# A decoder layer on one core: the residual kept by tokens, down and output projections with the weights as the moving operand

## The chip, the cores and the metric

One NeuronCore of one Trainium2 chip runs the kernel. The metric is the device time of one execution in microseconds; three runs are shown, and their median counts. Besides the runs there is one profiled execution, from which all rows come.

## The reference

256 tokens (T), model width 2048 (D), feed-forward width 5632 (FF), 16 heads of 128, all float32:

```python
x = x + 0.5 * swiglu(rms_norm(x, ffn1_norm), w_gate1, w_up1, w_down1)
h = rms_norm(x, mix_norm);  z = h @ w_in            # q|k|v|B|C|xt|gate_attn|gate_conv
y_a = moba(q, k, v) @ w_attn_out                    # 256 tokens are one block: plain causal ALiBi attention
y_c = (B * causal_conv3(C * xt)) @ w_conv_out
x = x + (sigmoid(g_a) * y_a + sigmoid(g_c) * y_c) @ w_out
x = x + 0.5 * swiglu(rms_norm(x, ffn2_norm), w_gate2, w_up2, w_down2)
out = rms_norm(x, final_norm)
swiglu(h, g, u, d) = (silu(h @ g) * (h @ u)) @ d
```

## The kernel before, in words

Everything is kept transposed: `x` is [128, 16, 256], 16 tiles of 128 features by 256 tokens. Weights (some 460 MB) come from HBM once, in chunks of 512 KB: 128 partitions by 1024 numbers (CK = 8 K tiles of 128 outputs).

Each operand of a product is cut into a part rounded to the type float32r and a rest. `cut` does it for a weight chunk: ScalarE casts `w` to `hi` (L509), VectorE writes `lo = w - hi` (L510). For the activations `split_col` writes both parts side by side into 512 columns: `xn` (normed x), `at` (attention output) and `ring` (hidden activations of the feed-forward blocks, and the inputs of `wco` and `wo`).

- `job` (L158, L159) computes one tile of 128 outputs by 256 tokens. For each K tile: the stationary `hi` times all 512 columns (main part and correction), then the stationary `lo` times the first 256.
- `v_step` (L372 to L374) does the other form, since attention needs v by tokens: for each K tile and each 128 tokens the rounded activations are stationary and 512 columns of `hi`, then of `lo`, stream by; then the activations' rest is stationary with `hi` again. It has two banks of PSUM.
- `ffn` walks three rounds of hidden tiles, ROUNDS = (0,12), (12,28), (28,44): gate and up jobs fill `ring`, then 16 down jobs per round add half their result to `x[:, m, :]`. In the last round `finish_x` squares the tile for the next norm and splits it into `xn`.
- `mixer` runs the conv part, `conv_out`, attention (`v_step`, `stage_qk`, `stage_t`, `stage_pv`), `attn_out`, and 16 jobs of `wo`.
- `norm_cols` sums the squares over features with matmuls against `ones` (L121) and forms 1/sqrt; `norm_row` spreads that along the free axis. The factor is applied after the next matmul.

The order is written out by hand: `steps` is a list, and the loop at the end issues it. For each chunk it issues loads up to 7 chunks ahead on SP's queue (five `w` buffers), cuts up to 4 ahead (four `hi`, four `lo`), then the chunk's matmuls, and then one entry of `pending`, the post-processing of the job before. A step without chunks and without a `hold` flushes all of `pending` first:

```python
if not n:
    if s.hold is None:
        flush()
    s.pe(None)
    continue
```

One such step stands at the second tile of a last round and loads ScalarE's table for Sqrt.

Of the kernel before, what the change touches and what calls it, by code (L numbers as in the profile page):

```python
# [8 lines left out]
F32 = mybir.dt.float32  # L9
# [5 lines left out]
P = 128  # L15
# [9 lines left out]
ROUNDS = ((0, 12), (12, 28), (28, 44))  # L25
RING = 18
LOAD_AHEAD = 6
SPLIT_AHEAD = 4
NEG = -3.0e38

G1, GM, G2, GF, BG, CV = 0, 16, 32, 48, 64, 96
NCST = 144


class Step:
    def __init__(self, chunks, pe, post=None, hold=None):
        self.hold = hold
        self.chunks = chunks
        self.pe = pe
        self.post = post  # L40


@with_exitstack
def macaron_kernel(ctx: ExitStack, tc: tile.TileContext, xT, cst, wg1, wu1, wd1, win, wv, wao,
                   wco, wo, wg2, wu2, wd2, out):
# [69 lines left out]
    def norm_cols(tag):
        """1 / sqrt(mean(x^2) + eps) of token i * 128 + p in rcol[tag][p, i]."""
        ps = patt.tile([P, 4 * P], F32, name="psS", tag="psS")
        a = acc.pop(tag)
        for i in range(2):
            for j, t in enumerate(a):  # L120
                nc.tensor.matmul(ps[:, i:i + 1], t[:, i * P:(i + 1) * P], ones, start=(j == 0), stop=(j == 1))  # L121
# [92 lines left out]
    def prepare(k0, k1):  # L214
        for k in range(k0, k1):
            split_col(xn[:, k, :], x[:, k, :], vec(G1, k))

    def ffn(tag, wg, wu, wd, gain_next, next_tag, first=False):
# [4 lines left out]
        def gu(t):  # L223
# [27 lines left out]
        for r, (k0, k1) in enumerate(ROUNDS):  # L251
# [5 lines left out]
            last = r == len(ROUNDS) - 1  # L257
            for m in range(ND):
                def post(ps, m=m, last=last):
                    c = tmp("c")  # L260
                    nc.scalar.mul(c, ps[:, T:2 * T], 0.5)
                    nc.vector.tensor_add(c, c, x[:, m, :])
                    nc.vector.scalar_tensor_tensor(x[:, m, :], ps[:, 0:T], 0.5, c, op0=ALU.mult, op1=ALU.add)  # L263
                    if last:
                        finish_x(m, gain_next, next_tag)
                src = wd[m][:, k0 * P:k1 * P]
                nk = k1 - k0
                ch = [(src[:, k * P:min(k + CK, nk) * P], min(CK, nk - k)) for k in range(0, nk, CK)]
                if last and m == 1:
                    steps.append(Step([], lambda _: nc.scalar.preload_act_table(AF.Sqrt)))  # L270
                steps.append(job((tag, "d", r, m), ch, lambda k, k0=k0: ring((k0 + k) % RING), post))

    def finish_x(m, gain, tag):
        add_square(tag, m)
        if tag == "fin":
            nc.vector.tensor_scalar(sacc[:, m, :], x[:, m, :], vec(GF, m), None, op0=ALU.mult)
        else:
            split_col(xn[:, m, :], x[:, m, :], vec(gain, m))

    def mixer(gain_next, next_tag):  # L280
# [79 lines left out]
        def v_step(g):  # L360
# [18 lines left out]
            def post():  # L379
# [97 lines left out]

        for m in range(ND):
            def post(ps, m=m):
                c = tmp("c")  # L480
                nc.scalar.copy(c, ps[:, T:2 * T])
                nc.vector.tensor_add(c, c, x[:, m, :])
                nc.vector.tensor_add(x[:, m, :], ps[:, 0:T], c)
                finish_x(m, gain_next, next_tag)
            if m == 1:
# [93 lines left out]
_INS = ["xT", "cst", "wg1", "wu1", "wd1", "win", "wv", "wao", "wco", "wo", "wg2", "wu2", "wd2"]  # L579

# [35 lines left out]
```

## Time and profile before

| | us |
|---|---|
| median of 3 runs | 2513.7 |
| lowest and highest | 2513.22, 2515.71 |
| span of the profiled execution | 2511.6 |
| TensorE busy in that span | 2488.0 |

The span runs from the first to the last instruction of the profiled execution; the median stands 2.1 us above it. Spans of single matmuls are modelled and overlap, so the length of a stretch is read from where it begins and ends, not from the sum of its instructions.

### The profile page before, as it was taken

Reading aid. Unit: us, or ns where it says so; the run is one execution under the profiler, and the core shown is the slowest. Engines: PE = TensorE matmul, PEld = TensorE weight load, DVE = VectorE, ACT = ScalarE, POOL = GpSimd, SP = SyncE. Lnnn points to the kernel's source line nnn. Section 1 sums busy time; section 2 is a strip of 40 time slices with the busy share of each in tenths; the row PEclk is TensorE's granted clock in tenths of the full one; section 3 lists DMA queues with packets and bytes.
Section 4 is the critical chain, followed back from the end, with each engine's and each line's share of the span. In section 5 each row is a group of like instructions: output and inputs, shape, how many; then the busy total and the mean of one; then the engine's idle time right before and its main releaser. Section 6 shows DMA issues by size and latency. Waiting matters only on the chain.

```text
span 2511.6 us, 36296 instructions
## 1 busy us (share of the span) xinstructions
PE 2488.0 (99%) x14176; PEld 2181.3 (87%) x14176; DVE 1629.1 (65%) x2364; ACT 1206.7 (48%) x1807; POOL 1.9 (0%) x10
## 2 busy tenths in 40 slices
PE   8999999999999999999999999999999999999998
PEld 7888888888888888888888888888888888888886
DVE  6766666566677777655555566667666666656666
ACT  5544444444554444444444454455544444444443
POOL 0000000000000000000000000000000000000000
PEclk9999999999999999999999999999999999999999
DMA  6556566655665565556555545555555655656563
GB/s 219 196 177 205 185 192 190 188 187 191 188 189 185 185 198 189 192 187 190 177 169 183 168 164 192 189 188 189 186 192 171 204 189 191 190 187 191 187 189 121
DMA packets 131932, 468.02 MB, mean 186 GB/s; under 512 B 14640, under 2 KB 14768, under 8 KB 131760
## 3 DMA queue, kind: packets, MB, share of 16 engines
q1 hardware_dynamic: 131760, 465.70, 58.1%
q8 instruction: 111, 1.82, 0.3%
q14 instruction: 61, 0.50, 0.1%
HBM read 463.54 MB, written 2.10 MB: 185 GB/s over the span
## 4 chain that ended last, share of the span: by engine, by line
PE 98%; DVE 1%; DMA 1%; issue 0%; ACT 0%; SPq 0%; DVEq 0%; ACTq 0%
PE ps L158 62%; PE ps L159 32%; PE pv L374 1%; PE pv L373 1%; PE pv L372 1%; DMA w<-in_wu 0%; DMA w<-in_wg 0%; PE psS L395 0%; PE psV L429 0%; DVE lo L510 0%; PE psT L417 0%; DVE sacc L572 0%; PE psS L394 0%; PE psV L430 0%; PE psS L121 0%
## 5 line engine op out<-in xcount | busy, mean ns | idle before, releaser
L158 PE MATMUL ps<-xn,hi 128*128 128x512 f32 x4544 | 1583.6, 393 | 0.0
L510 DVE TENSOR_TENSOR lo<-w,hi 128x1024 fp32r<-128x1024 f32 (+1 forms) x904 | 1075.0, 1196 | 715.4 <-ACT hi L509 714.8
L159 PE MATMUL ps<-xn,lo 128*128 128x256 f32 x4544 | 1270.2, 280 | 0.0
L509 ACT CAST hi<-w 128x1024 fp32r<-128x1024 f32 (+1 forms) x904 | 921.6, 1024 | 605.5 <-PE ps L158 290.3
L158 PEld LDWEIGHTS ps<-xn,hi 128*128 128x128 f32 x4544 | 853.2, 188 | 187.5
L159 PEld LDWEIGHTS ps<-xn,lo 128*128 128x128 f32 x4544 | 853.1, 188 | 0.5
L158 PE MATMUL ps<-ring,hi 128*128 128x512 f32 x1920 | 674.9, 393 | 0.0
L159 PE MATMUL ps<-ring,lo 128*128 128x256 f32 x1920 | 543.0, 283 | 0.0
L158 PEld LDWEIGHTS ps<-ring,hi 128*128 128x128 f32 x1920 | 360.6, 188 | 83.3
L159 PEld LDWEIGHTS ps<-ring,lo 128*128 128x128 f32 x1920 | 360.9, 188 | 0.0
L172 DVE TENSOR_TENSOR t<-ps,c 128x256 f32<-128x256 f32 x320 | 133.9, 418 | 23.1 <-ACT c L170 23.1
L170 ACT COPY c<-ps 128x256 f32<-128x256 f32 x320 | 116.2, 363 | 54.5 <-PE ps L159 54.5
L87 ACT CAST ring<-hh 128x256 fp32r<-128x256 f32 x88 | 35.8, 407 | 200.3 <-DVE hh L235 200.3
L228 ACT ACTIVATE silu<-t 128x256 f32<-128x256 f32 x88 | 36.8, 418 | 157.3 <-DVE t L226 157.3
L158 PE MATMUL ps<-at,hi 128*128 128x512 f32 x256 | 89.5, 392 | 0.0
L159 PE MATMUL ps<-at,lo 128*128 128x256 f32 x256 | 71.6, 280 | 0.0
L88 DVE TENSOR_TENSOR ring<-hh,ring 128x256 fp32r<-128x256 f32 x88 | 37.5, 426 | 41.7 <-ACT ring L87 41.7
L110 ACT ACTIVATE sq<-x 128x256 f32<-128x256 f32 x56 | 22.3, 414 | 75.8 <-DVE x L263 50.1
L158 PEld LDWEIGHTS ps<-at,hi 128*128 128x128 f32 x256 | 48.1, 188 | 10.6
L374 PE MATMUL pv<-hi,xn 128*128 128x512 f32 x128 | 50.9, 398 | 0.0
L372 PE MATMUL pv<-hi,xn 128*128 128x512 f32 x128 | 50.7, 396 | 0.0
L373 PE MATMUL pv<-lo,xn 128*128 128x512 f32 x128 | 50.4, 394 | 0.0
(87 smaller groups left out, 850.3 us busy)
## 6 DMA issues: line engine op xcount, KB each, us to landing
w<-in_win SPq DMA_DIRECT2D x224, 512.0 KB, 4.0
w<-in_wg SPq DMA_DIRECT2D x172, 512.0 KB, 3.9
w<-in_wu SPq DMA_DIRECT2D x172, 512.0 KB, 3.8
w<-in_wd SPq DMA_DIRECT2D x160, 512.0 KB, 3.8
w<-in_wco SPq DMA_DIRECT2D x32, 512.0 KB, 3.9
w<-in_wv SPq DMA_DIRECT2D x32, 512.0 KB, 4.2
w<-in_wao SPq DMA_DIRECT2D x32, 512.0 KB, 4.2
w<-in_wo SPq DMA_DIRECT2D x32, 512.0 KB, 3.9
```

The costliest lines, as they stand in the source:

```text
L87: nc.scalar.copy(dst[:, 0:T], src)
L88: nc.vector.tensor_sub(dst[:, T:2 * T], src, f32(dst[:, 0:T]))
L158: nc.tensor.matmul(ps, hi[:, j * P:(j + 1) * P], r, start=(k == 0), stop=False)
L159: nc.tensor.matmul(ps[:, 0:T], lo[:, j * P:(j + 1) * P], r[:, 0:T], start=False, stop=(k == n - 1))
L170: nc.scalar.copy(c, ps[:, T:2 * T])
L172: nc.vector.tensor_add(t, ps[:, 0:T], c)
L228: nc.scalar.activation(s, g, AF.Silu)
L372: nc.tensor.matmul(pv[i], xh, hi[:, cols], start=(k == 0), stop=False)
L373: nc.tensor.matmul(pv[i], xh, lo[:, cols], start=False, stop=False)
L374: nc.tensor.matmul(pv[i], xl, hi[:, cols], start=False, stop=(k == ND - 1))
L509: nc.scalar.copy(hi[:, 0:nk * P], w)
L510: nc.vector.tensor_sub(lo[:, 0:nk * P], w, f32(hi[:, 0:nk * P]))
```

## The change

- `x` becomes token-major, [128, 2, 2048]. The transposed x that the first norm needs is loaded into `sacc`; the token-major one comes later, in four DMAs behind weight chunks 24, 26, 28 and 30.
- The down projections and `wo` no longer use `job` but `wide_job`: the form of `v_step`, four blocks (NB) of 512 outputs per round, `ring` stationary, the weights' `hi` and `lo` moving. Their weights are laid out for that in HBM (`blocks`), as `wv` is already.
- `residual` adds a block to `x` and squares it with `accum_out` (`row_square`), so that `norm_cols` sums rows on VectorE for the two inner norms and the final one. `turn` transposes a block of x back on TensorE, 8 transposes per block, and splits it into `xn`; the final norm needs none.
- The output is written by tokens, in four DMAs; the final gain comes as rows (`load_gain`, one buffer).
- Tiles are padded and shifted: `pad`, `padw`, a larger `ones`, T + 8 in `tmp`, chunks of 1024 + 128 numbers. Chunks for `job` start 24 numbers (96 bytes) into their `hi` and `lo`, chunks for `wide_job` and `v_step` at 0. `tmp` has 8 buffers instead of 10, `ring` 17 instead of 18. The first job after each change of `xn` has chunks of 4 K tiles.

The diff, cut to its core:

```diff
-RING = 18
+NW = 4 * P
+NB = D // NW
+X_LOAD = 24
+RING = 17
...
-G1, GM, G2, GF, BG, CV = 0, 16, 32, 48, 64, 96
-NCST = 144
+G1, GM, G2, BG, CV = 0, 16, 32, 48, 80
+NCST = 128
+LINE = 32
+SHIFT = 24
...
+    const.tile([P, 3 * LINE], F32, name="pad")
+    x = const.tile([P, 2, D], F32, name="x")
     xn = const.tile([P, ND, 2 * T], F32R, name="xn")
     at = const.tile([P, ND, 2 * T], F32R, name="at")
     sacc = const.tile([P, ND, T], F32, name="sacc")
+    xin = sacc
+    yout = sacc.rearrange("p a b -> p (a b)").rearrange("p (a b) -> p a b", b=D)
     cs = const.tile([P, NCST], F32, name="cs")
-    ones = const.tile([P, 1], F32, name="ones")
+    ones = const.tile([P, 4 * LINE], F32, name="ones")[:, 0:1]
     ident = const.tile([P, P], F32, name="ident")
     dist = const.tile([P, 3 * P], F32, name="dist")
+    work.tile([P, LINE], F32, name="padw", tag="padw", bufs=1)
...
-        t = work.tile([P, T + 2], F32, name=name, tag="tmp", bufs=10)
+        t = work.tile([P, T + 8], F32, name=name, tag="tmp", bufs=8)
...
+    ssq = {}
+    def row_square(tag, i, nb, junk):
+        if tag not in ssq:
+            ssq[tag] = work.tile([P, 2, NB], F32, name="ssq", tag="ssq", bufs=2)
+        nc.scalar.activation(junk, x[:, i, nb * NW:(nb + 1) * NW], AF.Square,
+                             accum_out=ssq[tag][:, i, nb:nb + 1])
...
+        if tag in acc:
...
+        else:
+            nc.vector.reduce_sum(s, ssq.pop(tag), axis=AX.X)
+            total = s
+        nc.vector.tensor_scalar(v, total, 1.0 / D, EPS, op0=ALU.mult, op1=ALU.add)
...
-    def pieces(w, m, nk=ND):
-        return [(w[m][:, k * P:min(k + CK, nk) * P], min(CK, nk - k)) for k in range(0, nk, CK)]
+    def pieces(w, m, ck=CK):
+        return [(w[m][:, k * P:(k + ck) * P], ck) for k in range(0, ND, ck)]
+    def wide(w, nb, k0=0, k1=ND):
+        return [(w[nb][:, k * NW:(k + 2) * NW], CK) for k in range(k0, k1, 2)]
...
+    def wide_job(chunks, src, post):
+        n = 2 * len(chunks)
+        held = []
+        def pe(parts):
+            pv = [psum_big("pv0"), psum_big("pv1")]
+            held.extend(pv)
+            k = 0
+            for hi, lo, _ in parts:
+                for j in range(2):
+                    cols = slice(j * NW, (j + 1) * NW)
+                    a = src(k)
+                    for i in range(2):
+                        xh = a[:, i * P:(i + 1) * P]
+                        xl = a[:, T + i * P:T + (i + 1) * P]
+                        nc.tensor.matmul(pv[i], xh, hi[:, cols], start=(k == 0), stop=False)
+                        nc.tensor.matmul(pv[i], xh, lo[:, cols], start=False, stop=False)
+                        nc.tensor.matmul(pv[i], xl, hi[:, cols], start=False, stop=(k == n - 1))
+                    k += 1
+                yield
+        return Step(chunks, pe, [lambda q=q: q(held) for q in post], shift=0)
+    def turn(nb, gain):
+        for half, tag in ((0, "psT"), (1, "psV")):
+            ps = patt.tile([P, 4 * P], F32, name=tag, tag=tag)
+            for c in range(2):
+                m = nb * 4 + half * 2 + c
+                for i in range(2):
+                    nc.tensor.transpose(ps[:, c * T + i * P:c * T + (i + 1) * P], x[:, i, m * P:(m + 1) * P], ident)
+                split_col(xn[:, m, :], ps[:, c * T:(c + 1) * T], vec(gain, m))
+    def residual(nb, factor, tag, gain):
+        cols = slice(nb * NW, (nb + 1) * NW)
+        def add(pv):
+            for i in range(2):
+                if factor is None:
+                    nc.vector.tensor_add(x[:, i, cols], pv[i], x[:, i, cols])
+                else:
+                    nc.vector.scalar_tensor_tensor(x[:, i, cols], pv[i], factor, x[:, i, cols],
+                                                   op0=ALU.mult, op1=ALU.add)
+                if tag is not None:
+                    row_square(tag, i, nb, pv[i])
+                if tag == "fin":
+                    nc.vector.tensor_mul(yout[:, i, cols], x[:, i, cols], grow[nb])
+        if tag is None or tag == "fin":
+            return [add]
+        return [add, lambda pv: turn(nb, gain)]
+    grow = {}
+    def load_gain(nb):
+        grow[nb] = work.tile([P, NW], F32, name="grow", tag="grow", bufs=1)
+        nc.sync.dma_start(grow[nb], gf[:, nb * NW:(nb + 1) * NW])
...
-            steps.append(job((tag, "g", t), pieces(wg, t), rhs, post_g))
+            steps.append(job((tag, "g", t), pieces(wg, t, CK if t else CK // 2), rhs, post_g))
...
-            for m in range(ND):
...
-                        finish_x(m, gain_next, next_tag)
...
+            for nb in range(NB):
+                if last and nb == 1:
                     steps.append(Step([], lambda _: nc.scalar.preload_act_table(AF.Sqrt)))
-                steps.append(job((tag, "d", r, m), ch, lambda k, k0=k0: ring((k0 + k) % RING), post))
-
-    def finish_x(m, gain, tag):
-        add_square(tag, m)
-        if tag == "fin":
-            nc.vector.tensor_scalar(sacc[:, m, :], x[:, m, :], vec(GF, m), None, op0=ALU.mult)
-        else:
-            split_col(xn[:, m, :], x[:, m, :], vec(gain, m))
+                if last and next_tag == "fin":
+                    steps.append(Step([], lambda _, nb=nb: load_gain(nb), hold=False))
+                steps.append(wide_job(wide(wd, nb, k0, k1), lambda k, k0=k0: ring((k0 + k) % RING),
+                                      residual(nb, 0.5, next_tag if last else None, gain_next)))
...
-            steps.append(job(("win", part, c), pieces(win, part * ND + c), rhs, post))
+            steps.append(job(("win", part, c), pieces(win, part * ND + c, CK // 2 if (part, c) == (4, 0) else CK),
+                             rhs, post))
...
-            return Step(chunks, pe, post)
+            return Step(chunks, pe, post, shift=0)
...
-        for m in range(ND):
...
+        for nb in range(NB):
+            if nb == 1:
                 steps.append(Step([], lambda _: nc.scalar.preload_act_table(AF.Sqrt)))
-            steps.append(job(("o", m), pieces(wo, m), lambda k: ring(k), post))
+            steps.append(wide_job(wide(wo, nb), ring, residual(nb, None, next_tag, gain_next)))
...
+    chunks = [c + (s.shift,) for s in steps for c in s.chunks]
...
             raw.append(w)
+            q = len(raw) - X_LOAD
+            if q in (0, 2, 4, 6):
+                cols = slice(q * T, (q + 2) * T)
+                nc.sync.dma_start(x[:, :, cols], xt[:, :, cols])
...
+            _, nk, off = chunks[len(split)]
             w = raw[len(split)][:, 0:nk * P]
-            hi = hpool.tile([P, CW], F32R, name="hi", tag="hi")
-            lo = lpool.tile([P, CW], F32R, name="lo", tag="lo")
-            nc.scalar.copy(hi[:, 0:nk * P], w)
-            nc.vector.tensor_sub(lo[:, 0:nk * P], w, f32(hi[:, 0:nk * P]))
+            hi = hpool.tile([P, CW + 4 * LINE], F32R, name="hi", tag="hi")[:, off:off + nk * P]
+            lo = lpool.tile([P, CW + 4 * LINE], F32R, name="lo", tag="lo")[:, off:off + nk * P]
+            nc.scalar.copy(hi, w)
+            nc.vector.tensor_sub(lo, w, f32(hi))
             split.append((hi, lo, nk))
...
+    nc.sync.dma_start(xin[:, 0:2, :], xT[:, 0:2, :])
...
     norm_cols("fin")
-    r = norm_row("fin")
-    for m in range(ND):
-        nc.vector.tensor_mul(sacc[:, m, :], sacc[:, m, :], r[:, 0:T])
-        if m in (1, 3, 7, 11, 15):
-            a = {1: 0, 3: 2}.get(m, m - 3)
-            nc.sync.dma_start(out[:, a:m + 1, :], sacc[:, a:m + 1, :])
+    r = rcol["fin"]
+    for q in range(2):
+        cols = slice(q * D // 2, (q + 1) * D // 2)
+        nc.vector.tensor_scalar(yout[:, 0, cols], yout[:, 0, cols], r[:, 0:1], None, op0=ALU.mult)
+        nc.sync.dma_start(out[:, 0, cols], yout[:, 0, cols])
+        nc.scalar.activation(yout[:, 1, cols], yout[:, 1, cols], AF.Copy, scale=r[:, 1:2])
+        nc.sync.dma_start(out[:, 1, cols], yout[:, 1, cols])
...
+    def blocks(w):
+        w = np.asarray(w).reshape(w.shape[-2:])
+        k, n = w.shape
+        w = w.reshape(k // P, P, n // NW, NW).transpose(2, 1, 0, 3)
+        return np.ascontiguousarray(w).reshape(n // NW, P, k // P * NW)
```

## Rows read from the trace of the kernel before

**Rows 1.** The page: span, busy time of each engine, clock granted to TensorE in 40 slices.

```profile
span 2511.6 us, 36296 instructions
...
PE 2488.0 (99%) x14176; PEld 2181.3 (87%) x14176; DVE 1629.1 (65%) x2364; ACT 1206.7 (48%) x1807; POOL 1.9 (0%) x10
...
PEclk9999999999999999999999999999999999999999
```

**Rows 2.** The page: the chain that ended last, shares of the span.

```profile
PE 98%; DVE 1%; DMA 1%; issue 0%; ACT 0%; SPq 0%; DVEq 0%; ACTq 0%
PE ps L158 62%; PE ps L159 32%; PE pv L374 1%; PE pv L373 1%; PE pv L372 1%; DMA w<-in_wu 0%; DMA w<-in_wg 0%; PE psS L395 0%; PE psV L429 0%; DVE lo L510 0%; PE psT L417 0%; DVE sacc L572 0%; PE psS L394 0%; PE psV L430 0%; PE psS L121 0%
```

**Rows 3.** Busy time by stretch: from:to and length, then each engine, clock, DMA.

```profile
core 0: us, PE busy (x) PEld busy (x) DVE busy (x) ACT busy (x) POOL busy (x), PEclk, DMA share, GB/s
161.81:229.23 67.42, 67.42 (x387) 59.09 (x385) 41.98 (x66) 32.02 (x49) 0.00 (x0) 1.00 0.60 192
229.23:406.72 177.49, 177.49 (x1026) 156.22 (x1025) 116.14 (x159) 85.38 (x127) 0.00 (x0) 1.00 0.60 192
406.73:496.60 89.87, 89.87 (x514) 78.76 (x513) 52.58 (x67) 38.38 (x49) 0.00 (x0) 1.00 0.62 189
...
1199.04:1221.44 22.40, 22.40 (x98) 18.03 (x97) 10.64 (x10) 8.66 (x9) 0.00 (x0) 1.00 0.57 189
...
2406.86:2496.74 89.88, 89.88 (x515) 78.78 (x514) 58.87 (x93) 41.67 (x62) 0.00 (x0) 1.00 0.49 148
```

**Rows 4.** Timeline behind the first down projections: start, length, engine, line, count.

```profile
758.32 0.97 PEld L121 LDWEIGHTS psS<-ones,acc 128*128 128x128 f32 x8
758.43 0.95 PE L121 MATMUL psS<-ones,acc 128*128 128x1 f32 x8
```

**Rows 5.** The chain in order of time: start, length (us), what, count.

```profile
758.59 0.79 PE psS L121 x8
759.38 0.34 PE ps L158
...
1244.47 0.33 PE psT L417 x3
1250.35 0.43 PE psV L429 x2
```

**Rows 6.** Groups by line: shapes, count, busy us, mean ns, idle before.

```profile
L510 DVE TENSOR_TENSOR lo<-w,hi 128x1024 fp32r<-128x1024 f32 (+1 forms) x904 | 1075.0, 1196 | 715.4 <-ACT hi L509 714.8
L509 ACT CAST hi<-w 128x1024 fp32r<-128x1024 f32 (+1 forms) x904 | 921.6, 1024 | 605.5 <-PE ps L158 290.3 <-issue 161.3 <-ACT hi L509 88.2
...
L263 DVE SCALAR_TENSOR_TENSOR x<-ps,c 128x256 f32<-128x256 f32 x96 | 40.8, 425 | 3.6
...
L90 ACT ACTIVATE xn<-x,cs 128x256 fp32r<-128x256 f32 x48 | 22.7, 495 | 1.9 <-DMA cs<-in_cst 1.8
...
L398 DVE SCALAR_TENSOR_TENSOR s<-dist,psS 128x384 f32<-128x384 f32 x16 | 8.7, 545 | 0.0
...
L276 DVE TENSOR_SCALAR sacc<-x,cs 128x256 f32<-128x256 f32 x16 | 5.6, 348 | 0.1
```

**Rows 7.** Timeline of the tail, TensorE's last weight matmul to the output DMAs.

```profile
2496.62 0.28 PE L159 MATMUL ps<-ring,lo 128*128 128x256 f32 x1
...
2496.94 0.38 ACT L261 ACTIVATE c<-ps 128x256 f32<-128x256 f32 x1 [3.79 <-PE ps L159]
...
2499.68 0.16 DVE L124 TENSOR_SCALAR rc<-psS 128x2 f32<-128x2 f32 x1 [0.98 <-PE psS L121]
...
2500.90 0.16 DVE L130 TENSOR_TENSOR rc<-rc 128x2 f32<-128x2 f32 x1
...
2503.16 4.97 SPq L575 DMA_DIRECT2D out_y<-sacc  x5
```

**Rows 8.** DMA queue and issues by line: count, KB each, median us to landing.

```profile
q1 hardware_dynamic: 131760, 465.70, 58.1%
...
out_y<-sacc SPq DMA_DIRECT2D x3, 512.0 KB, 2.6
```

More of the change, by code (lines that the diff above doesn't have):

```diff
@@ L29, with __init__ @@
 NEG = -3.0e38
-G1, GM, G2, GF, BG, CV = 0, 16, 32, 48, 64, 96
-NCST = 144
+G1, GM, G2, BG, CV = 0, 16, 32, 48, 80
+NCST = 128
+LINE = 32
+SHIFT = 24
 class Step:
-    def __init__(self, chunks, pe, post=None, hold=None):
+    def __init__(self, chunks, pe, post=None, hold=None, shift=SHIFT):
         self.hold = hold
+        self.shift = shift
         self.chunks = chunks
@@ L43, in macaron_kernel @@
 @with_exitstack
-def macaron_kernel(ctx: ExitStack, tc: tile.TileContext, xT, cst, wg1, wu1, wd1, win, wv, wao,
+def macaron_kernel(ctx: ExitStack, tc: tile.TileContext, xT, xt, gf, cst, wg1, wu1, wd1, win, wv, wao,
                    wco, wo, wg2, wu2, wd2, out):
@@ L106, in add_square @@
             acc.setdefault(tag, []).append(t)
-            nc.scalar.activation(t, x[:, m, :], AF.Square)
+            nc.scalar.activation(t, xin[:, m, :], AF.Square)
         else:
             sq = tmp("sq")
-            nc.scalar.activation(sq, x[:, m, :], AF.Square)
+            nc.scalar.activation(sq, xin[:, m, :], AF.Square)
             nc.vector.tensor_add(acc[tag][0], acc[tag][0], sq)
     R, rcol = {}, {}
-    def norm_cols(tag):
[L117 to L121, printed above, removed]
+    ssq = {}
[4 more added lines that the diff above has]
+                             accum_out=ssq[tag][:, i, nb:nb + 1])
+    def norm_cols(tag):
         r = work.tile([P, 8], F32, name="rc", tag="rc", bufs=2)
         v, s, y = r[:, 0:2], r[:, 2:4], r[:, 4:6]
-        nc.vector.tensor_scalar(v, ps[:, 0:2], 1.0 / D, EPS, op0=ALU.mult, op1=ALU.add)
+        if tag in acc:
+            ps = patt.tile([P, 4 * P], F32, name="psS", tag="psS")
+            a = acc.pop(tag)
+            for i in range(2):
+                for j, t in enumerate(a):
+                    nc.tensor.matmul(ps[:, i:i + 1], t[:, i * P:(i + 1) * P], ones, start=(j == 0), stop=(j == 1))
+            total = ps[:, 0:2]
+        else:
+            nc.vector.reduce_sum(s, ssq.pop(tag), axis=AX.X)
+            total = s
+        nc.vector.tensor_scalar(v, total, 1.0 / D, EPS, op0=ALU.mult, op1=ALU.add)
         nc.scalar.activation(s, v, AF.Sqrt)
@@ new lines, in turn @@
+    def turn(nb, gain):
[9 more added lines that the diff above has]
+        def add(pv):
+            for i in range(2):
+                if factor is None:
[10 more added lines that the diff above has]
+        return [add, lambda pv: turn(nb, gain)]
@@ L215, in prepare @@
         for k in range(k0, k1):
-            split_col(xn[:, k, :], x[:, k, :], vec(G1, k))
+            split_col(xn[:, k, :], xin[:, k, :], vec(G1, k))
     def ffn(tag, wg, wu, wd, gain_next, next_tag, first=False):
@@ L257, in ffn @@
             last = r == len(ROUNDS) - 1
-            for m in range(ND):
[L259 to L264, printed above, removed]
-                        finish_x(m, gain_next, next_tag)
[L266 to L269, printed above, removed]
-                    steps.append(Step([], lambda _: nc.scalar.preload_act_table(AF.Sqrt)))
-                steps.append(job((tag, "d", r, m), ch, lambda k, k0=k0: ring((k0 + k) % RING), post))
-    def finish_x(m, gain, tag):
-        add_square(tag, m)
-        if tag == "fin":
-            nc.vector.tensor_scalar(sacc[:, m, :], x[:, m, :], vec(GF, m), None, op0=ALU.mult)
-        else:
-            split_col(xn[:, m, :], x[:, m, :], vec(gain, m))
+            for nb in range(NB):
+                if last and nb == 1:
+                    steps.append(Step([], lambda _: nc.scalar.preload_act_table(AF.Sqrt)))
+                if last and next_tag == "fin":
+                    steps.append(Step([], lambda _, nb=nb: load_gain(nb), hold=False))
+                steps.append(wide_job(wide(wd, nb, k0, k1), lambda k, k0=k0: ring((k0 + k) % RING),
+                                      residual(nb, 0.5, next_tag if last else None, gain_next)))
     def mixer(gain_next, next_tag):
@@ L476, in mixer @@
                 gate_job(6, m + 3)
-        for m in range(ND):
[L479 to L485, printed above, removed]
+        for nb in range(NB):
+            if nb == 1:
                 steps.append(Step([], lambda _: nc.scalar.preload_act_table(AF.Sqrt)))
-            steps.append(job(("o", m), pieces(wo, m), lambda k: ring(k), post))
+            steps.append(wide_job(wide(wo, nb), ring, residual(nb, None, next_tag, gain_next)))
     ffn("f1", wg1, wu1, wd1, GM, "mix", first=True)
     mixer(G2, "f2")
-    ffn("f2", wg2, wu2, wd2, GF, "fin")
-    chunks = [c for s in steps for c in s.chunks]
+    ffn("f2", wg2, wu2, wd2, None, "fin")
+    chunks = [c + (s.shift,) for s in steps for c in s.chunks]
     raw, split = [], []
@@ L497, in load @@
         while len(raw) < min(n, len(chunks)):
-            src, nk = chunks[len(raw)]
+            src, nk, _ = chunks[len(raw)]
             w = wpool.tile([P, CW], F32, name="w", tag="w")
@@ L514, in macaron_kernel @@
     nc.scalar.preload_act_table(AF.Sqrt)
-    nc.sync.dma_start(x[:, 0:2, :], xT[:, 0:2, :])
-    nc.sync.dma_start(cs, cst)
+    nc.sync.dma_start(xin[:, 0:2, :], xT[:, 0:2, :])
+    nc.sync.dma_start(cs[:, 0:NCST], cst)
     load(1)
-    nc.sync.dma_start(x[:, 2:4, :], xT[:, 2:4, :])
+    nc.sync.dma_start(xin[:, 2:4, :], xT[:, 2:4, :])
     load(2)
     for i in range(1, 4):
-        nc.sync.dma_start(x[:, 4 * i:4 * i + 4, :], xT[:, 4 * i:4 * i + 4, :])
+        nc.sync.dma_start(xin[:, 4 * i:4 * i + 4, :], xT[:, 4 * i:4 * i + 4, :])
         load(min(LOAD_AHEAD, 2 + 2 * i))
@@ L594, in tiles @@
         return np.ascontiguousarray(w.reshape(k // P, P, n // P, P).transpose(2, 1, 0, 3)).reshape(n // P, P, k)
-    w0 = np.asarray(w_in)[0]
-    wv = w0[:, 2 * D:3 * D].reshape(ND, P, 4, 4 * P).transpose(2, 1, 0, 3)
+    def blocks(w):
[3 more added lines that the diff above has]
+        return np.ascontiguousarray(w).reshape(n // NW, P, k // P * NW)
     arrays = {
         "xT": np.ascontiguousarray(np.asarray(x)[0].T.reshape(ND, P, T).transpose(1, 0, 2)),
+        "xt": np.ascontiguousarray(np.asarray(x)[0].reshape(2, P, D).transpose(1, 0, 2)),
+        "gf": np.ascontiguousarray(np.broadcast_to(np.asarray(final_norm).reshape(1, D), (P, D))),
         "cst": np.ascontiguousarray(np.concatenate(
-            [cols(ffn1_norm), cols(mix_norm), cols(ffn2_norm), cols(final_norm), cols(b_gate),
+            [cols(ffn1_norm), cols(mix_norm), cols(ffn2_norm), cols(b_gate),
              np.asarray(conv_w)[0].reshape(3, ND, P).transpose(2, 1, 0).reshape(P, 3 * ND)], axis=1)),
-        "wg1": tiles(ffn1_w_gate), "wu1": tiles(ffn1_w_up), "wd1": tiles(ffn1_w_down),
-        "win": tiles(w_in), "wv": np.ascontiguousarray(wv).reshape(4, P, ND * 4 * P),
-        "wao": tiles(w_attn_out), "wco": tiles(w_conv_out), "wo": tiles(w_out),
-        "wg2": tiles(ffn2_w_gate), "wu2": tiles(ffn2_w_up), "wd2": tiles(ffn2_w_down),
+        "wg1": tiles(ffn1_w_gate), "wu1": tiles(ffn1_w_up), "wd1": blocks(ffn1_w_down),
+        "win": tiles(w_in), "wv": blocks(np.asarray(w_in)[0][:, 2 * D:3 * D]),
+        "wao": tiles(w_attn_out), "wco": tiles(w_conv_out), "wo": blocks(w_out),
+        "wg2": tiles(ffn2_w_gate), "wu2": tiles(ffn2_w_up), "wd2": blocks(ffn2_w_down),
     }
@@ L609 @@
     args = [nc.dram_tensor(f"in_{n}", arrays[n].shape, F32, kind="ExternalInput").ap() for n in _INS]
-    args.append(nc.dram_tensor("out_y", (P, ND, T), F32, kind="ExternalOutput").ap())
+    args.append(nc.dram_tensor("out_y", (P, 2, D), F32, kind="ExternalOutput").ap())
     with tile.TileContext(nc) as tc:
@@ L614 @@
     y = r.results[0]["out_y"]
-    return np.ascontiguousarray(y.transpose(2, 1, 0)).reshape(1, T, D)
+    return np.ascontiguousarray(y.transpose(1, 0, 2)).reshape(1, T, D)
```

4 lines of the change are left out of this document (1 added, 3 removed).

## The prediction

> **What bounds the kernel now.** I read the page's head first: TensorE is busy for 2488.0 us of 2511.6 and its clock is granted in full in all 40 slices [rows 1]. Busy time alone can mislead, so next the chain that ended last: 98% of it is TensorE, nearly all in the two matmul lines of `job`, L158 and L159 [rows 2]. So only what changes TensorE's stream, or the head and the tail, changes the time. VectorE and ScalarE split each weight chunk in 1.20 and 1.02 us [rows 6], where TensorE takes 2.8 us for a chunk, and the 16 DMA engines are 58% busy with the weight queue [rows 8]. These are the cover for everything that I cost at nothing below.
>
> Then the table by stage [rows 3]. The reader is to see the length of each stretch, since TensorE has no idle time in any. A pair is one K tile of `job`: a matmul of 512 columns and one of 256, each with its own weight load.
> - Gate and up jobs (moving operand `xn`): 177.49 us for 512 pairs, 346.7 ns each.
> - Down projections and `wo` (moving operand `ring`): 1664 pairs in seven stretches, two like 161.81:229.23 and five like 406.73:496.60 and 2406.86:2496.74: 2 x 67.42 + 5 x 89.88 = 584.2 us, 351.1 ns each.
> - One `v_step`, already in the form that the change spreads: 96 matmuls of 512 columns in 22.40 us, 233.3 ns each.
>
> **The stream, replaced.** Per K tile and 512 outputs, before: four pairs, 4 x 768 = 3072 columns and 8 weight loads, 1404 ns. After: six matmuls of 512, again 3072 columns, but 6 loads. At `v_step`'s own price that is 6 x 233.3 = 1400 ns: as good as nothing. So all hangs on what one such matmul will cost, and the trace of before has no row of just the new kind. What differs is the place of the operands. Tile sizes, added up in the order of allocation (each rounded up to 32 bytes), put `hi`, `lo` and `ring` 96 bytes past `xn`, counted modulo 128. So the gate and up pairs stream from offset 0 (346.7 ns), the `ring` pairs from offset 96 (351.1), `v_step` from 96 as well (233.3). After the change, with its pads, `ring`, `xn` and the wide chunks all lie at 0 modulo 512, and the narrow chunks stay at 96 by SHIFT.
>
> Two accounts fit the `xn` row. By loads: 768 columns at 2.4 GHz, the granted level in that row, are 320.0 ns, the other 26.7 belong to two loads, 13.3 each; then a 512-column matmul costs 213.3+13.3 = 226.7 ns. By columns: 346.7 x 512/768 = 231.1 ns. For the second speaks that `ring` and `v_step`, both streaming from 96, cost the same per column (0.457 and 0.456 ns) with unequal numbers of loads. For the first speaks that eight loads beside one-column matmuls came 0.11 us apart [rows 4], which is more than the 107 ns of a 256-column stream at that clock and half of a 512-column one: the short matmul, which the change takes out, is the one that a load can hold up. A fp32 matmul of 256 columns has hardly any excess, two in 0.43 us [rows 5]: 215 ns. I take the first account, 226.7, and keep 231.1, 233.3 and 215 as bounds.
>
> The Trainium skill (TensorE: Matmul & The Clock Gate, section on the back-to-back issue gap) gives the isolated gap of a warm 512-column matmul as N/2.4 + 2.5 = 215.8 ns, and its step-by-step section says that loading the next weights takes no read bandwidth from the running matmul. The 233.3 ns row of `v_step` disagrees, so no number here stands on it; by it, an estimate, the sum below would be -45.5 us.
>
> **The sum, against the span of 2511.6 us.**
> - a) 416 K-tile groups (2 x 44 x 4 of the down projections, 16 x 4 of `wo`) x 6 = 2496 matmuls x 226.7 ns = 565.8, against 584.2: -18.4.
> - b) `v_step`, 384 matmuls, 233.3 to 226.7: -2.6. Its chunks move to offset 0.
> - c) `conv_out`, 256 narrow pairs on `ring`, which moves to offset 0: 351.1 to 346.7, -1.1.
> - d) `turn`: 32 fp32 transposes in each of two stages, new on TensorE. Three such took 0.33 us on the chain [rows 5], so 64 x 0.11 = +7.0. They wait for nothing where they are queued behind two chunks (5.4 us) of the next wide job; each add takes about 0.67 us (256 columns 0.425, 384 columns 0.545 [rows 6], carried on).
> - e) The exception is block 1 of a last round: the step that preloads the Sqrt table flushes all posts, so the first block's transposes stand right behind its last matmul and wait for both adds. The eviction starts about 0.04 us after that matmul's end [rows 7]; 0.39+0.04+1.33+0.06 less the 0.23 at which the next would have started is 1.6 us, twice (into the mixer, into the second block; the final norm has no `turn`): +3.2. Behind the waiting transposes the whole next wide job is queued, nobody else.
> - f) `norm_cols` for two inner norms loses its eight matmuls: 0.79 us, and 0.34 in place of 0.23 for the matmul behind them [rows 5]: -1.8. `reduce_sum` on VectorE takes their place, under the held posts.
> - g) Tail. Before, 6.5 us from the start of the last weight matmul to the first output DMA (2496.62 to 2503.16), 8.4 more to the end [rows 7]. After: 0.4 until the add starts, two adds and two gain products of 0.67, a sum over `ssq` of about 0.35, the small norm steps (2499.68 to 2501.06, 1.4), one scaling of 1024 columns (1.1 to 1.4, from L276's 0.348 for 256 [rows 6]), so 5.9 to 6.2; the same 2 MB then go out in four DMAs. Between -3.5 (all four issued early, last one landing in its 2.6 us [rows 8]) and +0.7; I take -0.5, since 2 MB moved in 8.4 us before.
>
> Nothing for: the 2 MB of token-major x (four DMAs on SP's queue between weight chunks 24 and 31, so that weights queue behind each) and the 1 MB of gains, hidden behind five `w` buffers of 2.7 us each and the DMA engines' free 42%; if that cover failed, four DMAs of 512 KB at 2.6 us [rows 8] would be the price, 10 us. Nothing for `tmp` with 8 buffers in place of 10, `ring` with 17 (a round holds 16 and one ahead), the halved first chunks, the squares on ScalarE, which has 0.5 of its time free. The last block's `turn` is due before K tile 12 of the next job, two 4-tile chunks after its add; ScalarE and VectorE need four steps of about 0.5 us [rows 6], so I expect under 1 us there.
>
> Sum: -18.4-2.6-1.1+7.0+3.2-1.8-0.5 = -14.2, a span of 2497.4. The median of the runs is 2.1 us above this profiled span (2513.7), so 2499.5 us.
>
> **The rivals.** c) to g) together are +6.8 in each.
> - Columns, not loads: 231.1 ns. a) -7.4, b) -0.8, +6.8 = -1.4: 2512.3 us, no change. At `v_step`'s 233.3 it is -1.9+6.8 = +4.9: 2518.6. For it: the equal price per column at offset 96. Against: those rows stream from 96, and `v_step` loads its weights from 0, which no narrow row does.
> - Slower: the narrow pairs slip. All tiles move, and the 4864 narrow pairs on `xn` and `at` could fall from 346.7 to the 351.1 that the same code takes on `ring`: +21.4, c) lost, so +8.3: 2522.0 us. It decides from 3.0 ns per pair (14.2/4864), and is slower beyond 0.2% from 4.0. Against: narrow `hi` keeps its 96 bytes to `xn`.
> - Loads at nothing: 215 ns as in fp32. a) -47.6, b) -7.0, +6.8 = -47.8: 2465.9 us. The Trainium skill's 215.8 (the same section) would be nearly this. Against: no float32r row comes near it.
>
> **How the numbers follow.** A measurement tells 0.2%, about 5 us, from no change. Forecast 0.52 and loads at nothing 0.10, both faster; columns 0.24, the same; slip 0.14, slower. So faster 0.62, same 0.24, slower 0.14. Half the way to the columns' price, either side of 226.7 (224.4 to 228.9), is 2493 to 2506, the forecast's own range. The whole range, 2484 to 2519, takes in the columns' case at both prices and leaves out loads at nothing and the slip (most of it), about 2 in 10.
>
> **What would show it.** In the stage table, each down stretch of 64 groups (two thirds of the rounds) should shrink from 89.9 to 87.0 us, and `v_step` from 22.40 to 21.8; the gate and up stretches should stay at 346.7 per pair. `psT`/`psV` transposes should total 7 us, with two waits of about 1.6 us on VectorE's `x`. The prediction is wrong if the wide matmuls start 231 ns or more apart, if the narrow pairs change, or if TensorE waits at the wide blocks' borders.

## The result: slower by 0.84%

The changed kernel takes 2535.7 us (median of 4 runs, 2535.3 to 2536.5), the kernel before 2514.5 in the same session. The ratio is 1.0084, interval 1.0070 to 1.0098. The forecast was 2499.5 us, range 2484 to 2519. The profiled span is 2533.5 us where 2497.4 was worked out: 36.1 us are to be found.

### The profile page after: what moved, and what is told of

It reads as the page before. It is cut to its first block, busy times and chain, and to the rows that moved or that the text cites. A ratio compares the mean times of both kernels' runs of the same rounds, so it can differ in the third digit from the quotient of the medians.

```text
span 2533.5 us, 34394 instructions
## 1 busy us (share of the span) xinstructions
PE 2485.4 (98%) x13380; PEld 2148.9 (85%) x13380; DVE 1557.4 (61%) x2123; ACT 1175.2 (46%) x1685; POOL 1.9 (0%) x10
## 4 chain that ended last, share of the span: by engine, by line
PE 96%; DVE 2%; ACT 1%; DMA 1%; issue 0%; SPq 0%; ACTq 0%; DVEq 0%
PE ps L183 46%; PE ps L184 23%; PE pv L222 7%; PE pv L224 7%; PE pv L223 7%; PE pv L447 1%; PE pv L445 1%; PE pv L446 1%; ACT hi L580 1%; DVE lo L581 1%; DVE xn L102 1%; DMA w<-in_wg 0%; ACT pv L132 0%; PE psV L502 0%; PE psS L468 0%
## 5 line engine op out<-in xcount | busy, mean ns | idle before, releaser
L222 PE MATMUL pv<-hi,ring 128*128 128x512 f32 x832 | 327.1, 393 | 0.0
L223 PE MATMUL pv<-lo,ring 128*128 128x512 f32 x832 | 326.1, 392 | 0.0
L224 PE MATMUL pv<-hi,ring 128*128 128x512 f32 x832 | 326.0, 392 | 0.0
L224 PEld LDWEIGHTS pv<-hi,ring 128*128 128x128 f32 x832 | 157.6, 189 | 33.1
L223 PEld LDWEIGHTS pv<-lo,ring 128*128 128x128 f32 x832 | 157.8, 190 | 32.7
L222 PEld LDWEIGHTS pv<-hi,ring 128*128 128x128 f32 x832 | 157.8, 190 | 32.8
L183 PE MATMUL ps<-ring,hi 128*128 128x512 f32 x256 | 89.4, 392 | 0.0
L184 PE MATMUL ps<-ring,lo 128*128 128x256 f32 x256 | 71.6, 280 | 0.0
L183 PEld LDWEIGHTS ps<-ring,hi 128*128 128x128 f32 x256 | 48.1, 188 | 10.6
```

The source lines that it names most:

```text
L183: nc.tensor.matmul(ps, hi[:, j * P:(j + 1) * P], r, start=(k == 0), stop=False)
L184: nc.tensor.matmul(ps[:, 0:T], lo[:, j * P:(j + 1) * P], r[:, 0:T], start=False, stop=(k == n - 1))
L222: nc.tensor.matmul(pv[i], xh, hi[:, cols], start=(k == 0), stop=False)
L223: nc.tensor.matmul(pv[i], xh, lo[:, cols], start=False, stop=False)
L224: nc.tensor.matmul(pv[i], xl, hi[:, cols], start=False, stop=(k == n - 1))
```

## The profile after

The page of the changed kernel, its head and its chain:

```profile
span 2533.5 us, 34394 instructions
...
PE 2485.4 (98%) x13380; PEld 2148.9 (85%) x13380; DVE 1557.4 (61%) x2123; ACT 1175.2 (46%) x1685; POOL 1.9 (0%) x10
...
PE 96%; DVE 2%; ACT 1%; DMA 1%; issue 0%; SPq 0%; ACTq 0%; DVEq 0%
PE ps L183 46%; PE ps L184 23%; PE pv L222 7%; PE pv L224 7%; PE pv L223 7%; PE pv L447 1%; PE pv L445 1%; PE pv L446 1%; ACT hi L580 1%; DVE lo L581 1%; DVE xn L102 1%; DMA w<-in_wg 0%; ACT pv L132 0%; PE psV L502 0%; PE psS L468 0%
```

TensorE is busy 2.6 us less than in [rows 1], in a span that is 21.9 us longer. The share of other engines in the chain has grown from 1% to 3% [rows 2], with a new name among them: VectorE's `xn` at L102, the second half of `split_col`. The table by stretch, which answers to [rows 3], says where:

```profile
core 0: us, PE busy (x) PEld busy (x) DVE busy (x) ACT busy (x) POOL busy (x), PEclk, DMA share, GB/s
162.72:228.03 65.31, 65.31 (x290) 54.06 (x289) 35.01 (x35) 25.87 (x26) 0.00 (x0) 1.00 0.64 196
228.03:405.53 177.50, 177.50 (x1026) 156.23 (x1024) 115.59 (x158) 85.07 (x126) 0.00 (x0) 1.00 0.58 189
405.53:492.60 87.07, 87.07 (x387) 72.08 (x385) 44.81 (x43) 34.31 (x34) 0.00 (x0) 1.00 0.65 195
659.00:781.12 122.12, 109.77 (x487) 89.67 (x485) 59.41 (x74) 52.10 (x75) 0.00 (x0) 0.94 0.52 156
685.59:688.90 3.31, 3.31 (x10) 2.64 (x10) 0.56 (x2) 2.80 (x3) 0.00 (x0) 0.50 0.00 0
744.12:746.90 2.78, 2.78 (x9) 2.20 (x8) 1.44 (x2) 1.41 (x2) 0.00 (x0) 0.50 0.00 0
770.64:774.20 3.56, 3.56 (x13) 3.08 (x12) 1.71 (x2) 2.19 (x3) 0.00 (x0) 0.50 0.00 0
1213.84:1235.63 21.79, 21.79 (x99) 18.03 (x97) 10.65 (x10) 8.69 (x9) 0.00 (x0) 1.00 0.59 197
1682.48:1804.88 122.40, 110.06 (x486) 89.74 (x485) 59.83 (x74) 52.09 (x75) 0.00 (x0) 0.94 0.52 156
2434.37:2521.21 86.84, 86.84 (x386) 71.89 (x384) 45.19 (x47) 36.13 (x44) 0.00 (x0) 1.00 0.49 163
```

The first, third and last of these are down projections without `turn`: 65.31, 87.07 and 86.84 us. 288 and 384 matmuls of 512 columns make that 226.8, 226.7 and 226.1 ns each: the forecast's 226.7. `v_step` takes 21.79 us (21.8 was said), and the gate and up stretch is where it was, 177.50. The stretches 659.00:781.12 and 1682.48:1804.88 hold the wide jobs with `turn` and the first jobs behind them. Of these stretches they are the only ones in which TensorE is not busy from end to end (109.77 of 122.12), and in which the granted clock falls to 0.50, that is 1.2 GHz. The three short rows are pieces of the first one, 2.8 to 3.6 us long, in which it streams at that clock.

The timeline of the second block's `turn`, with the columns start, length, engine, line, operation, and in brackets the idle time before it and what ended it:

```profile
714.49 0.38 PE L236 MATMUL psT<-ident,x 128*128 128x128 f32 x2
...
714.91 0.47 ACT L101 ACTIVATE xn<-psT,cs 128x256 fp32r<-128x256 f32 x1 [0.43 <-PE psT L236]
715.65 0.48 DVE L102 SCALAR_TENSOR_TENSOR xn<-psT,cs,xn 128x256 fp32r<-128x256 f32 x1
...
716.18 0.44 PE L236 MATMUL psT<-ident,x 128*128 128x128 f32 x2 [1.31 <-DVE xn L102]
...
716.46 0.38 PE L236 MATMUL psV<-ident,x 128*128 128x128 f32 x2
...
718.10 0.44 PE L236 MATMUL psV<-ident,x 128*128 128x128 f32 x2 [1.26 <-DVE xn L102]
```

Two transposes go into `psT`, then TensorE waits until ScalarE and VectorE have split that tile, then come the next two. The same happens in `psV`. The waits of the first of the two stretches, in all (who waits, who ended it, then the sum in us, the count and the longest):

```profile
PE psT L236 <- DVE xn L102: 6.9, 4, 3.0
PE psV L236 <- DVE xn L102: 4.9, 4, 1.3
PE psT L236 <- DVE x L248: 0.6, 2, 0.3
```

12.4 us of waits and 9.65 us at half the clock, of which half is lost (4.8): some 17 us in each of the two stretches. What the prediction did foresee, the wait for the adds behind the flush (`x` L248), is the smallest row.

## The experiments

Theory A: the second tile of a half is transposed into the same PSUM tile that is being split, and that makes the wait. Theory B: the splits are simply late, behind the next chunks' `hi` and `lo` on ScalarE and VectorE, and TensorE meets them in any order.

**e1_grouped.** Both tiles of a half are transposed, then both are split.

```diff
                 for i in range(2):
                     nc.tensor.transpose(ps[:, c * T + i * P:c * T + (i + 1) * P], x[:, i, m * P:(m + 1) * P], ident)
+            for c in range(2):
+                m = nb * 4 + half * 2 + c
                 split_col(xn[:, m, :], ps[:, c * T:(c + 1) * T], vec(gain, m))
```

> In turn, both tiles of a half are transposed before either is split; nothing else. Theory A (the second tile's transposes wait because they write the same PSUM tile that ScalarE and VectorE are still reading): the 16 waits of 1.3 to 3 us on VectorE's xn (13.9 + 9.7 us) go, and with them most of the half-clock matmuls behind them (some 8 us), so about 30 us less than the changed kernel: 2505 us, under the kernel before. Theory B (the splits are late because they stand behind the next chunks' hi and lo on ScalarE and VectorE, and TensorE meets them in any order): the waits only move, to the next turn or to the first job that reads xn, and the time stays within 8 us of 2535.

2503.4 us, ratio to the kernel before 0.9952 (0.9937 to 0.9967). The waits and the stretch that answers to 659.00:781.12:

```profile
PE ps L183 <- DVE xn L102: 1.8, 3, 1.0
PE psT L236 <- DVE x L250: 0.6, 2, 0.3
```

```profile
658.63:764.36 105.73, 103.40 (x487) 85.50 (x485) 58.60 (x74) 51.45 (x75) 0.00 (x0) 1.00 0.57 176
```

All waits for the splits inside `turn` are gone, the clock stays at 1.00, and the stretch is 16.4 us shorter. That is 33.5 us on the span, from 2533.5 to 2500.0. B has nothing for it: the splits are still where they were in the queues of ScalarE and VectorE. What is left of B is the first row, 1.8 us at the first job that reads the last block.

**e5_own_tiles.** The order of the changed kernel, but each tile of a block in a PSUM tile of its own.

```diff
             for c in range(2):
+                if half and c:
+                    ps = psum_big("psB")
+                else:
+                    own = ("psT", "psV", "psS")[2 * half + c]
+                    ps = patt.tile([P, 4 * P], F32, name=own, tag=own)
                 m = nb * 4 + half * 2 + c
```

> The changed kernel with turn's order kept (two transposes, split, two transposes, split), but each of the four tiles of a block in a PSUM tile of its own; the flushing step stays. Theory A, in the form that the shared PSUM tile makes the wait: the same as e1, 2503 us, within 3. If it is the order that matters (a split between two transposes on the engines' queues): no better than the changed kernel, 2535 us.

2499.8 us, ratio 0.9941 (0.9923 to 0.9959). The order was not at fault, the shared tile was. It is 3.6 us under e1, 1.9 by the profiled spans. That would fit the point of e7 below: the first tile of a half is split one pair of transposes sooner, and the waits at the first job fall from 1.8 us in three to 1.0 in one. This was not tried by itself.

```profile
PE ps L183 <- DVE xn L102: 1.0, 1, 1.0
PE psT L240 <- DVE x L252: 0.6, 2, 0.3
```

**e2_grouped_noflush.** e1, and the Sqrt preload does not flush, neither in `ffn` nor in `mixer`.

```diff
-                    steps.append(Step([], lambda _: nc.scalar.preload_act_table(AF.Sqrt)))
+                    steps.append(Step([], lambda _: nc.scalar.preload_act_table(AF.Sqrt), hold=False))
...
-                steps.append(Step([], lambda _: nc.scalar.preload_act_table(AF.Sqrt)))
+                steps.append(Step([], lambda _: nc.scalar.preload_act_table(AF.Sqrt), hold=False))
```

> As e1, and the two steps that preload the Sqrt table no longer flush the posts before them, so the first block's turn also stands behind two chunks of the next wide job. Theory A, with step e) of the prediction: 3 to 5 us less than e1, about 2501 us. If the flush costs nothing once the waits inside turn are gone: the same as e1.

2501.1 us, ratio 0.9944 (0.9929 to 0.9959): 2.3 us under e1. The stretch that answers to e1's 658.63:764.36:

```profile
659.45:764.20 104.75, 102.98 (x487) 85.55 (x485) 58.60 (x74) 51.44 (x75) 0.00 (x0) 1.00 0.58 177
```

It is 0.98 us shorter, and there are two of them, so the flush costs some 2.0 us, less than the 3.2 of step e).

**e7_pair.** e2, and the first two jobs behind a changed `xn` run side by side, 4 K tiles of the one and 4 of the other.

```diff
-            steps.append(job((tag, "g", t), pieces(wg, t, CK if t else CK // 2), rhs, post_g))
...
             if t == 0:
+                steps.append(pair_job(wg, 0, wu, 0, rhs, post_g, post_u))
                 steps.append(norms[0])
+                return
```

`pair_job` takes its chunks from both weights in turn and has a PSUM tile for each; the mixer's first two jobs are joined in the same way.

> e2, with the first two jobs behind each change of xn side by side, 4 K tiles of one and 4 of the other in turn, so that K tiles 12 to 15 are due after 8.3 us instead of 4.2. If the waits there are the late splits of the last block: they go, twice 2.7 us, 2496 us. If not: 2501 us as e2.

2496.1 us, ratio 0.9922 (0.9905 to 0.9940), the best of the kernels here that compute the whole layer: 5.0 us under e2, 4.2 by the profiled spans. No wait of TensorE is left from 640 to 800 us. In e2 the first job reaches K tile 12 after 4.2 us (12 pairs of 346.7 ns), and the last block's add, turn and splits need more than that.

**e6_no_turn.** e2 without `turn`; the mixer and the second block read an old `xn`.

```diff
-        return [add, lambda pv: turn(nb, gain)]
+        return [add, lambda pv: None]
```

> e2 without turn: the inner blocks of x are neither transposed nor split, so the mixer and the second block read an old xn. It leaves out 64 transposes and 32 splits. By the prediction's step d) 7.0 us for the transposes, and by e2's profile some 5 us of waits at the first job behind each last block: 12 us less than e2, 2489 us. If the wait at the first job comes from its weight chunks and not from the splits: 7 us less, 2494 us.

2486.8 us, 14.3 less than e2 (12 were expected). The last round of the first block with transposes (e2) and without; the third row, of e6, answers to e2's 659.45:764.20 above:

```profile
659.45:749.23 89.78, 89.78 (x410) 74.57 (x409) 48.20 (x55) 42.65 (x59) 0.00 (x0) 1.00 0.59 178
```

```profile
657.42:744.49 87.07, 87.07 (x387) 72.08 (x385) 43.22 (x43) 37.96 (x47) 0.00 (x0) 1.00 0.61 183
657.42:756.06 98.64, 98.64 (x455) 82.21 (x453) 51.75 (x58) 45.09 (x59) 0.00 (x0) 1.00 0.62 186
```

Three of the four turns fall into this stretch: 2.71 us for 24 transposes, 0.113 us each. So a round with hidden turns costs 89.78 us, where the narrow jobs before took 89.87 to 89.88 [rows 3]: the wide form there gains nothing. With the jobs behind the last block the stretch is 104.75 us in e2 and 98.64 in e6, 6.11 less, and 12.2 for the two stretches: 7.2 us for 64 transposes, and 5.0 for the waits at the first jobs. The rest of the 14.3 had come before any turn: e6 reached 657.42 where e2 reached 659.45, 2.0 us apart. Most of that is the clock at the start: from 38.50 to 41.80 us it stood at 0.50 in e2 and at 0.86 on average in e6.

**e4_before_places.** The kernel before, with only the places of its tiles changed (pads, SHIFT, `v_step`'s chunks at 0, `ring` 17, `tmp` 8).

```diff
+    const.tile([P, 3 * LINE], F32, name="pad")
     x = const.tile([P, ND, T], F32, name="x")
...
-    cs = const.tile([P, NCST], F32, name="cs")
-    ones = const.tile([P, 1], F32, name="ones")
+    cs = const.tile([P, 8 * LINE], F32, name="cs")
+    ones = const.tile([P, 4 * LINE], F32, name="ones")[:, 0:1]
...
+    work.tile([P, 48], F32, name="padw", tag="padw", bufs=1)
...
+            hi = hpool.tile([P, CW + 4 * LINE], F32R, name="hi", tag="hi")[:, off:off + nk * P]
```

> The kernel before with only the places of its tiles changed: pads, SHIFT for narrow chunks, v_step's chunks at 0, ring with 17 and tmp with 8 buffers; no wide jobs. By offset: 1920 narrow pairs on ring fall from 351.1 to 346.7 ns (-8.4 us) and 384 matmuls of v_step from 233.3 to 226.7 (-2.6), about 2503 us. If offsets do nothing: 2514 us.

2503.2 us, ratio 0.9952 (0.9936 to 0.9969), with no wide job at all. The gate stretch and two rounds of narrow down jobs:

```profile
229.34:406.83 177.49, 177.49 (x1026) 156.28 (x1025) 116.10 (x159) 85.34 (x127) 0.00 (x0) 1.00 0.60 192
406.83:495.58 88.75, 88.75 (x515) 78.15 (x513) 52.59 (x67) 38.38 (x49) 0.00 (x0) 1.00 0.64 192
661.98:750.73 88.75, 88.75 (x515) 78.15 (x514) 64.59 (x96) 50.29 (x80) 0.00 (x0) 1.00 0.63 191
```

Pairs on `ring` now take 88.75/256 = 346.7 ns, as those on `xn` do. 11.7 us come from places alone.

**e3_wide_at_96.** e2 with the wide chunks 96 bytes into their tiles.

```diff
-        return Step(chunks, pe, [lambda q=q: q(held) for q in post], shift=0)
+        return Step(chunks, pe, [lambda q=q: q(held) for q in post], shift=SHIFT)
...
-            return Step(chunks, pe, post, shift=0)
+            return Step(chunks, pe, post, shift=SHIFT)
```

> As e2, but the chunks of wide_job and v_step start 96 bytes into hi and lo, like those of the narrow jobs. By offset (a moving operand 96 bytes off a 128-byte step costs 6.6 ns per 512 columns, as v_step had before): 2880 matmuls from 226.7 to 233.3, +19 us over e2. If the wide form is cheap by its number of loads alone, wherever the chunk lies: the same as e2.

2520.9 us, 19.8 over e2, ratio to the kernel before 1.0022 (1.0013 to 1.0031). A round without `turn`:

```profile
407.72:497.31 89.59, 89.59 (x387) 72.08 (x386) 44.76 (x43) 34.12 (x34) 0.00 (x0) 1.00 0.63 190
```

89.59/384 = 233.3 ns, `v_step`'s price in [rows 3]. The wide form itself is cheap only where its moving chunk lies well.

**e8_places_swept.** e2 with each job's chunks at another place.

```diff
+    places = {0: 0, SHIFT: 0}
+    for s in steps:
+        if s.chunks:
+            kind = s.shift
+            s.shift = 4 * (places[kind] % 32)
+            places[kind] += 1
```

> e2, with every step's chunks at another place in hi and lo: narrow jobs and wide jobs each walk through 0, 16, 32, ... 496 bytes. Its time as a whole says nothing; the length of each job does. By loads and offset: a wide job at 0 takes 226.7 ns per matmul and at 96 bytes 233.3; a narrow pair at 96 bytes 346.7. If 24 numbers is a good place for a stationary operand, other places are no better than 346.7 and some are worse; if the place of a stationary operand is of no account, all narrow jobs take 346.7 per pair.

One run, 2532.9 us. One job to a line: wide jobs at 0 and 16 bytes, then narrow jobs at 0, 16, 32, 64, 96, 112, 256 and 320, then wide jobs at 96 and 256.

```profile
162.56:178.90 16.34, 16.34 (x74) 13.52 (x73) 9.34 (x11) 6.89 (x8) 0.00 (x0) 1.00 0.68 197
178.90:195.58 16.68, 16.68 (x73) 13.54 (x72) 8.55 (x8) 6.29 (x6) 0.00 (x0) 1.00 0.66 193
279.71:285.26 5.55, 5.55 (x35) 4.86 (x34) 3.52 (x5) 2.67 (x4) 0.00 (x0) 1.00 0.57 195
285.26:290.82 5.56, 5.56 (x34) 4.89 (x33) 3.67 (x7) 2.68 (x4) 0.00 (x0) 1.00 0.61 192
290.82:296.37 5.55, 5.55 (x35) 4.88 (x33) 3.60 (x5) 2.67 (x4) 0.00 (x0) 1.00 0.55 174
301.92:307.57 5.65, 5.65 (x35) 4.92 (x34) 3.71 (x5) 2.67 (x4) 0.00 (x0) 1.00 0.58 191
313.20:318.76 5.56, 5.56 (x34) 4.89 (x33) 3.54 (x5) 2.68 (x4) 0.00 (x0) 1.00 0.51 157
318.76:324.41 5.65, 5.65 (x34) 4.93 (x33) 3.75 (x7) 2.67 (x4) 0.00 (x0) 1.00 0.65 212
369.30:374.85 5.55, 5.55 (x35) 4.85 (x33) 3.52 (x5) 2.68 (x4) 0.00 (x0) 1.00 0.56 194
145.72:151.36 5.64, 5.64 (x34) 4.90 (x33) 3.70 (x5) 2.67 (x4) 0.00 (x0) 1.00 0.61 176
452.95:475.35 22.40, 22.40 (x98) 18.02 (x97) 11.00 (x10) 8.38 (x8) 0.00 (x0) 1.00 0.65 188
1684.07:1705.89 21.82, 21.82 (x98) 18.02 (x97) 12.10 (x13) 10.28 (x11) 0.00 (x0) 1.00 0.67 195
```

Narrow jobs take 5.55 us (346.7 ns per pair) at the good places and 5.65 (353) at the worst ones, with others between. Of jobs with no other matmuls between theirs, those at each of the 16 places below 256 bytes take the same time, within 0.01 us, as those 256 bytes further; nothing goes below 346.6. For the wide job 0 is good (16.34 us for 72 matmuls, 226.9 ns) and so is 256 (21.82 for 96, 227.3); at 16 and 96 it takes 231.7 and 233.3 ns. So the 24 numbers (96 bytes) by which SHIFT moves narrow chunks are one of several good places for a stationary chunk, and 0 would do as well.

## Why the prediction was wrong

Step d) failed, in its words "They wait for nothing where they are queued behind two chunks (5.4 us) of the next wide job". It asked whether the adds would be done, and they were. It did not look at what the transposes write: the two tiles of a half share one PSUM tile, and the second pair was not written until the first had been read. Sixteen waits of 1.1 to 3.0 us, and the half clock that follows some of them, cost 33.5 us (e1; 35.4 by the span of e5). The row that gave the price, [rows 5], could not show such a wait: `stage_t` puts its three transposes into `psT` at a stretch and copies the tile once, behind the last.

Point by point:
- a) was right: 226.7 ns by loads (forecast 0.52), and not 231.1 by columns. Whether the 13.3 ns belong to the load or to each matmul no run can tell, since every matmul here has a load of its own. e3 and e4 show why `v_step` and `ring` had agreed per column: both streamed from a bad place. b) and c) were right as well: 21.79 us for a `v_step`, 346.7 ns for pairs on `ring` (the changed kernel's `conv_out`, and e4).
- d)'s price for a transpose was right, 0.113 us against 0.11 (e6). The last block of a stage, sized at "under 1 us" and put at nothing in the sum, is a second miss: it cost 2.5 us in each of the two stages (e6, and e7 got 5.0 back).
- e) was too dear: 2.0 us in all (e2) against 3.2. The adds start sooner, since the first bank is finished three matmuls before the last (the rows below).
- f) fits: the eight matmuls are gone, and TensorE waits for no `reduce_sum`. Of the terms at nothing, the loads of x and of the gains cost no wait of TensorE.
- g) was too dear too. The tail, from the start of the last weight matmul, is 12.3 us (2521.21 to 2533.5) against 15.0 before [rows 7]; -2.7 where -0.5 was taken:

```profile
2520.95 0.69 DVE L248 SCALAR_TENSOR_TENSOR x<-pv,x 128x512 f32<-128x512 f32 x1 [7.84 <-PE pv L224]
...
2521.21 0.39 PE L224 MATMUL pv<-hi,ring 128*128 128x512 f32 x1
...
2525.39 1.42 DVE L644 TENSOR_SCALAR sacc<-sacc,rc 128x1024 f32<-128x1024 f32 x2
2526.16 0.35 SPq L645 DMA_DIRECT2D out_y<-sacc  x1
```

The first output DMA starts 4.95 us after the last weight matmul, where 5.9 to 6.2 were worked out: the first add runs beside the last matmuls, and scaling 1024 columns took 0.75 us (two in 1.42, overlapping), not the 1.1 to 1.4 carried on from L276 [rows 6]. The output then takes 7.3 us to the end, against 8.4 before.

These add up: 33.5 for the shared tile, 5.0 for the last blocks, 0.2 for the transposes, less 1.2 for e) and 2.2 for g), are 35.3 of the 36.1 us to be found. Another 0.9 is there at the first wide job, which starts at 162.72 us where the first down job of before started at 161.81; runs with the same code up to there start it at 162.35 (e1) and 161.14 (e6).

The rivals: columns and loads at nothing are out by the 226.7. The Trainium skill's isolated gap of 215.8 ns (TensorE: Matmul & The Clock Gate, back-to-back issue gap) is out with them; no place of e8 comes near it. The 215 ns that the prediction took from a fp32 matmul was weak ground: [rows 5] has it for 256 columns, which at 2.4 GHz are 107 ns, so that row does not show a matmul without excess. The slip of narrow pairs did not happen, 177.50 us against 177.49, although e8 shows that it could have: at 112 bytes they cost 5.65 us a job. The sign came out on the side of a rival, but by no mechanism that was named there; only the last sign of being wrong, waits of TensorE at the wide blocks' borders, comes near it.

With `turn` mended the forecast would have held: e1 gives 2503.4 and e2 2501.1 for 2499.5. That it comes so close is partly luck, since the last blocks' 5.0 us, which the sum did not have, stand against the 3.4 by which e) and g) were too dear. And of the 18.8 us that e7 is ahead of its runs of the kernel before (2514.8), 11.7 are to be had by places alone (e4), with the old form. The wide form's own gain, -11.1 us for 2496 matmuls against narrow pairs at 346.7, is mostly paid back by the 7.2 us of transposes that it needs.

## What to carry to other kernels

When a step is given to a busy engine, ask not only whether its inputs are ready but who still reads what it writes: here two users of one PSUM tile in the order write, read, write, read made the writer wait for each reader, though they use different columns, and grouping the writes or giving each its own tile removed that. Whether the program asks for that wait tile by tile or the memory behind the tile needs it, no run tells. Waits of TensorE of little more than a microsecond, two in a row, cost its clock as well in three turns of four. Before a change of form is credited with a gain, change the places of the operands alone.

## What the runs showed of the hardware

- The speed of a float32r stream depends on where its operands lie: over 32 places of the stationary chunk of a narrow job 346.6 to 353.4 ns per pair, with a period of 256 bytes (e8), and per wide matmul 226.7 with the moving chunk at 0 (the changed kernel) and 233.3 with it at 96 bytes (e3).
- At the best places a stream costs its columns at 2.4 GHz plus 13.3 ns for each matmul with its weight load (768 columns in two matmuls 346.7, 512 in one 226.7). Loads beside one-column matmuls came 0.11 us apart [rows 4], about as long as a stream of 256 columns (107 ns) and half as long as one of 512, and the 13.3 ns are the same in both. Why they are left was not tried.
- The granted clock fell to 0.50 at three of the four turns of a last round. It fell behind the first and the third, each with waits of 1.3 us twice, about 0.7 us apart, and not behind the second (714.49), whose waits were as long, 1.31 and 1.26 us. In the fourth it had fallen by the end of the first wait, of 3.0 us: from 767.60 to 770.60 it stood at 0.50. In e3 it fell once (764.90 to 768.15) behind waits of 0.95, 0.41 and 0.41 us for the last block's splits; waits of 1.8 us in three at the same place left it at 1.00 in e1 and e2. What made the difference was not tried.
